# Padding two small resident tiles of an encoder trunk to multiples of 128 bytes

## The chip, the core and the metric

The kernel runs on one core of a Trainium2 chip. The metric is the device time of one execution in microseconds (us). Three runs of the kernel before took 3088.32, 3089.78 and 3091.51 us; their median, 3089.78, is its time. TensorE (PE in the profile) multiplies matrices, VectorE (DVE) and GpSimd (POOL) work element by element, ScalarE (ACT) applies functions and copies, SyncE (SP) issues most DMAs. On-chip tiles lie in SBUF, 128 partitions wide; results of TensorE land in PSUM.

## The reference, cut to what matters

Two layers over 256 tokens with 2048 features: a Conformer convolution module, then a bidirectional gated DeltaNet, each followed by a SwiGLU feed-forward of 5632 hidden units, with an RMSNorm ahead of each part and one at the end.

```python
def reference(x, ...):
    h = x
    for i in range(DEPTH):                      # 2
        hn = rmsnorm(h, mix_norm[i])
        if i == 0:
            mix = conformer_conv_module(hn, ...)   # pw1, GLU, 31-tap conv, LayerNorm, swish, pw2
        else:
            mix = gated_deltanet_bidir(hn, ...)    # one input product, scans both ways, out product
        h = h + mix
        h = h + swiglu_ffn(rmsnorm(h, ffn_norm[i]), w_gate_up[i], w_down[i])
    return rmsnorm(h, final_norm)

def swiglu_ffn(h, w_gate_up, w_down):
    gu = h @ w_gate_up
    gate, up = gu[..., :FFN_HIDDEN], gu[..., FFN_HIDDEN:]
    return (jax.nn.silu(gate) * up) @ w_down
```

Everything is float32.

## The kernel before, in words

**Products.** Features lie on partitions and tokens along the free axis, so an activation is a set of tiles of 128 features by 256 tokens. `products` (lines 163 to 196) computes blocks of 128 output features, over k-tiles of 128 input features. Weights come by DMA as `raw` tiles of eight k-tiles (line 149). For four k-tiles at a time ScalarE copies them into a `hi` tile of the type float32r (line 159), and VectorE writes the rest, `raw - hi`, into a `lo` tile (line 160). Activations are split in the same manner and lie as one tile `[hi | lo]` of 2 x 256 columns, 2048 bytes in a partition. For each k-tile TensorE then multiplies in one of two forms:

- *wide*: `lo` by the 256 columns of hi (line 184; line 187 in a block's first k-tile), `hi` by all 512 columns (line 185). Used by gate/up of both feed-forwards (activations `xs`, 88 blocks of 16 k-tiles in each layer), by down (`hs`, 16 blocks of 44), by pw2 (`y`, 16 blocks of 16) and by the DeltaNet's output product (`ys`, 16 blocks of 32).
- *narrow*: `hi` by hi, `hi` by lo, `lo` by hi, 256 columns each (lines 189, 190, 191). Used over `xs` by pw1 (32 blocks of 16) and the DeltaNet's input product (97 blocks of 16).

The weights are what TensorE holds; the activation tile is what streams through it, called the moving tile here.

**Order.** The tile framework's scheduler sets each engine's order and the waits. A wait orders a buffer's users: ScalarE, for one, writes a `hi` tile again once the last product that reads it is done. Four `hi` and four `lo` tiles go round, three `raw` tiles in the weights' pool and, during a feed-forward, three more in a pool of that phase, which every other chunk takes (lines 143 to 145).

**Where tiles lie.** Pools are laid out one behind the other in a partition, and tiles within a pool too, each rounded up to a multiple of 32 bytes. The first pool holds the constants (`cst_sb`, 1050 values, 4200 bytes, rounded to 4224) and the parameters of the features (`par_sb`, 499 values, 1996 bytes, rounded to 2016). 2016 is 32 more than a multiple of 64, so what follows begins at 32 modulo 64: the normed activations `xs`, the weights' pool (`raw`, `hi`, `lo`) and the first tiles of the small pool (`ss`, `rstd`, `warm`). `warm` (lines 244 to 247) is one value in a partition, 4 bytes rounded to 32: it brings what follows it back to 0 modulo 64. Its only use is to load a function's table on ScalarE early. Behind it lie `sq`, the residual stream `h` and the pools of each phase. Within the DeltaNet's pool a tile of 32 bytes, `rt`, makes most tiles behind it begin at 32 modulo 64.

Of the kernel before, what the change touches and what calls it, by code (L numbers as in the profile page):

```python
# [7 lines left out]
F32 = mybir.dt.float32  # L8
# [5 lines left out]
P = 128  # L14
# [9 lines left out]
CS = 4  # L24
NEG = -1.0e30
# PSUM banks
PSB = {"lin": 3, "sum": 1, "a": 1, "b": 2, "g": 1}
# [9 lines left out]
XB = 6  # L37
# taps of the depthwise convolution that GpSimd adds, by feature block
NPOOL = [15] * 12 + [14, 13, 6, 5]

# columns of the packed per-feature parameters
PAR = {}
# [9 lines left out]

# columns of the packed constants
CST = {}
# [12 lines left out]
def fv(ap, off, *dims):  # L67
    """A view of a tile by an offset and [stride, count] pairs over its free elements."""
    return bass.AP(ap.tensor, ap.offset + off, [list(ap.ap[0]), *[list(d) for d in dims]])


class Trunk:
    def __init__(self, ctx, tc, x, par, cst, pw1, pw2, win, wout, gu, dn, out):
        self.ctx, self.tc, self.nc = ctx, tc, tc.nc
        self.x, self.par_d, self.cst_d, self.out = x, par, cst, out
        self.pw1, self.pw2, self.win, self.wout, self.gu, self.dn = pw1, pw2, win, wout, gu, dn
        nc = self.nc
        pool = lambda name, **kw: ctx.enter_context(tc.tile_pool(name=name, bufs=1, **kw))
        self.cp = pool("const")
        self.xp = pool("acts")  # L80
        self.wp = pool("weights")
        self.sp = pool("small")
        self.ps = pool("psum", space=bass.MemoryType.PSUM)
        self.uid = 0
        self.pending = None
        self.ahead = self.more = None
        self.turn = False
        self.cst = self.cp.tile([P, NCST], F32, name="cst_sb")
        self.par = self.cp.tile([P, NRES], F32, name="par_sb")
        self.dram = pool("scratch", space=bass.MemoryType.DRAM)  # L90
        self.h_d = self.dram.tile([P, KD, S], F32, name="h_d")

    def new_h(self):
        """The residual stream on chip, in a pool of its own."""
        self.hs = ExitStack()
# [7 lines left out]
    def load_first(self, srcs):  # L103
        """The input and the first weights, in the order in which they are needed."""
        nc = self.nc
# [31 lines left out]

# [1 line left out]

    def raw_tile(self):  # L140
        """A chunk of weights; every other one from a phase that has room for more of them."""
        self.turn = not self.turn
# [3 lines left out]
    def raw_weights(self, src, k0, n):  # L146
        """n k-tiles of one column block."""
        raw = self.raw_tile()
        self.nc.sync.dma_start(raw[:, : n * P], src[:, k0 * P : (k0 + n) * P])
        return raw  # L150

    def halves(self, raw, i, n, pool=None):
        """k-tiles i to i + n as a high and a low part that float32r holds exactly."""
        nc = self.nc
# [8 lines left out]
    def products(self, srcs, kt, acts, wide=False, tags=("lin",), pool=None, order=None):  # L163
        """Blocks of 128 output features, k-tile by k-tile; acts: float32r tiles [P, hi | lo].

        order: of the k-tiles, within each CS of them."""
        nc = self.nc
# [37 lines left out]

# [1 line left out]

# [36 lines left out]
    def warm(self, func, after):  # L244
        """Loads a function's table on ScalarE, ahead of its use."""
        t = self.sp.tile([P, 1], F32, tag="warm", bufs=1, name=self.nm("warm"))
        self.nc.scalar.activation(t, after[:, :1], func)

# [9 lines left out]
    def norm_end(self):  # L258
        """The factor is traced behind the next product, whose result is the first to need it."""
        ss = [self.ss] if self.rest is None else [self.ss, self.rest]  # L260
        self.pending = lambda: self.rsqrt(self.token_sum(*ss), 1.0 / D, self.c("eps6"))

# [1 line left out]

    def conv_module(self, next_norm):
# [3 lines left out]
        with tc.tile_pool(name="conv", bufs=1, reuse_waits="tile") as cv:  # L269
# [27 lines left out]
            def add(key, t, n, last):  # L297
                """Sums over the channels, added up in PSUM."""
                if n == 0:
# [4 lines left out]
            def second(j):  # L304
                """The deviation from the first channels' mean, and its square's sum."""
                d = us[j]
# [64 lines left out]

            # mean = shift + dm: the first channels' deviations add up to nothing
            dm = new("dm", 1)
# [5 lines left out]
            lr = self.rsqrt(var, 1.0, self.c("eps5"), AF.Silu)  # L379
            # in the order in which VectorE and GpSimd get them done  # L380
            order = (0, 3, 1, 2, *range(4, KD))
# [21 lines left out]

# [1 line left out]

# [32 lines left out]

# [1 line left out]

    def deltanet(self, next_norm):
# [7 lines left out]
        G = NKH // 2  # L449
        # what the last heads leave early lies below what they need to the end  # L450
        with (tc.tile_pool(name="dn0", bufs=1, reuse_waits="tile") as d0,
# [23 lines left out]
        self.load_h(self.h_d)  # L475
        # the first lie within what dn0 leaves
        with (tc.tile_pool(name="out0", bufs=1, reuse_waits="tile") as o0,
# [15 lines left out]

    # tiles of the DeltaNet's pool: shape, number
    DN = {
# [33 lines left out]
    def dn_gates(self):  # L529
        """ln(beta) and the decays' sums within a block: as a token's scalars and along the tokens."""  # L530
        nc = self.nc
# [7 lines left out]
        V.tensor_scalar(m, y, 0.0, None, op0=ALU.max)  # L539
        # ln(1 + e) = 2 artanh(e / (2 + e))  # L540
        V.tensor_scalar(r, e, 2.0, None, op0=ALU.add)
# [41 lines left out]
    def short_conv(self, n):  # L583
        """Twice the SiLU of the five-tap convolution, of feature block n."""
        nc = self.nc
# [48 lines left out]
    def dn_front(self, g, qk):  # L634
        """Of four value heads, both ways: the masked, decayed products of keys with keys and with queries."""
        nc = self.nc
        xo, xd = self.d("xo"), self.d("xd")
        for h in range(2):
            q, k = qk[2 * h], qk[2 * h + 1]
            grams = []  # L640
            for x, tag in ((k, "kk"), (q, "kq")):
                ga = self.pst("g")
                # blocks of tokens ab, aa, bb, ba
                for i, (a, b) in enumerate(((0, 1), (0, 0), (1, 1), (1, 0))):
# [32 lines left out]
    def dn_lanes(self, xd):  # L677
        """Inverses of the 32 x 32 diagonal blocks of I + X, one block in a partition."""
        nc = self.nc
# [14 lines left out]
        at = lambda r, c: c * 32 + r  # L694
        # pairs of 1 x 1
        V.tensor_copy(fv(T, at(0, 1), (66, 16)), fv(L, at(0, 1), (66, 16)))
        # pairs of 2 x 2
        F = self.d("F")
# [8 lines left out]
        V.tensor_tensor(pj(T, 0, 3, (1, 2)), f(1, 0, (1, 2)), t0, op=ALU.add)  # L707
        # pairs of 4, 8 and 16
        for s in (4, 8, 16):
# [23 lines left out]
    def dn_inverse(self, g, xd, tt, tb):  # L733
        """The transposed inverses of the 128 x 128 triangular matrices from those of their diagonal blocks.

        One product serves both directions: what lies beside a diagonal block going forward and what lies
        beside it going backward are different blocks of one square. tt and tb hold the 32 x 32 inverses and
        their transposes; a matrix is counted by head and block of tokens (e), or by direction as well."""
        nc = self.nc
# [24 lines left out]

        # pairs of 32
        o = each(z32, lambda e: both(tt, e), 64)
# [7 lines left out]
        for d in range(2):  # L774
            V.transpose(fv(bl[rows(1 + d, 1)], 32 * d, (64, 8), (1, 32)), fv(o[rows(3 * d, 1)], 32 * d, (64, 8), (1, 32)))
        # pairs of 64
        o = each(z64, lambda e: bl[:, e * 64 : (e + 1) * 64], 64)
# [10 lines left out]
    def dn_heads(self, g, vs, xo, pb):  # L788
        """Four value heads: the solutions, and the normed outputs."""
        nc = self.nc  # L790
        blk = lambda t, m: t[:, m * P : (m + 1) * P]
        ot, os = [], self.d("os")
        for i in range(4):
            v = vs[i]
            # of pb: forward block a, forward block b, backward block a, backward block b
            inv = lambda m: blk(pb, 4 * i + m)
# [9 lines left out]

            # the first blocks (forward a, backward b), what they leave of the others, and those
            nc.scalar.copy(w1, two(w1, ((inv(0), blk(v, 0)), (inv(3), blk(v, 1)))))
# [3 lines left out]
            fa, ba, fb, bb = blk(w1, 0), blk(w2, 0), blk(w2, 1), blk(w1, 1)  # L812
            # ar: forward ab, aa, bb; backward aa, bb, ba
            o = self.pst("b")
# [94 lines left out]
def layout(i):  # L909
    """Arrays as the chip reads them: features on partitions, weights by blocks of 128 outputs."""  # L910
    import numpy as np
# [45 lines left out]
```

## Time and profile before

| What | Value |
|---|---|
| time, median of three runs | 3089.78 us |
| span of the profiled execution | 3092.0 us |
| TensorE busy | 2859.3 us, 92% of the span |
| VectorE busy | 2332.2 us, 75% |
| ScalarE busy | 1695.6 us, 55% |
| GpSimd busy | 1009.9 us, 33% |
| granted TensorE clock, mean over the span | 0.970 |
| bytes moved by DMA | 521.38 MB, mean 169 GB/s |

The profile was taken in an execution of its own, whose span from its first to its last instruction is 2.2 us longer than the median of the timed runs. A line such as "L185 PE MATMUL acc<-xs,hi 128*128 128x512 f32 x2816 | 982.0, 398 | 0.6 <-..." is a group: 2816 matmuls of line 185 that write `acc` and read `xs` and `hi`, 982.0 us busy in all, 398 ns the mean of one, then the engine's idle time just ahead of them and what ended it. Matmuls overlap each other, so their pitch (from one start to the next) is shorter than their duration; rates are read from starts.

### The profile page before, as it was taken

What the parts mean: (1) busy time and instruction counts of PE and PEld (TensorE: products, weight loads), DVE (VectorE), ACT (ScalarE), POOL (GpSimd) and SP (SyncE); (2) the same over time, 40 slices, a digit from 0 to 9 for tenths busy, and PEclk for the clock granted to TensorE, in tenths of its full rate; (3) what the DMA queues carried; (4) which work ended last, traced back from release to release, by engine and by line L of the source; (5) the groups of instructions that cost most, each with busy time, mean ns of one, the idle gap of its engine ahead of it and who ended that gap; (6) DMA issues with size and microseconds to landing.
All of it is one profiled execution on the core that took longest, in us unless ns stands there. A gap on an engine that the chain in (4) does not pass through costs nothing. (4 is left out here: it accounts for less than half of the span.)

```text
span 3092.0 us, 50294 instructions
## 1 busy us (share of the span) xinstructions
PE 2859.3 (92%) x18122; PEld 2566.7 (83%) x18122; DVE 2332.2 (75%) x3735; ACT 1695.6 (55%) x3449; POOL 1009.9 (33%) x1047
## 2 busy tenths in 40 slices
PE   7778799999999999878888889888999999999998
PEld 6777688888888889877888888888888888888887
DVE  8999876666666667899899997985766666666555
ACT  6665555555555445654665456554545555555443
POOL 6777420000000111566667766562110000000111
PEclk9999899999999999999999999999999999999999
DMA  4333266555556665543544445456666555556664
GB/s 164 121 112 103 89 202 189 188 185 188 186 186 193 197 200 166 181 150 115 164 155 149 137 144 166 129 158 200 192 189 209 185 187 188 185 187 184 192 190 141
DMA packets 163866, 521.38 MB, mean 169 GB/s; under 512 B 18240, under 2 KB 34944, under 8 KB 163616
## 3 DMA queue, kind: packets, MB, share of 16 engines
q1 hardware_dynamic: 162320, 516.86, 52.7%
q8 instruction: 142, 2.33, 0.3%
q10 hardware_dynamic: 1296, 1.30, 0.1%
q14 instruction: 108, 0.88, 0.1%
HBM read 497.02 MB, written 21.07 MB: 168 GB/s over the span
## 5 line engine op out<-in xcount | busy, mean ns | idle before, releaser
L160 DVE TENSOR_TENSOR lo<-raw,hi 128x512 fp32r<-128x512 f32 x1764 | 1384.7, 788 | 644.6 <-ACT hi L159 638.3
L159 ACT CAST hi<-raw 128x512 fp32r<-128x512 f32 x1764 | 1085.9, 619 | 935.4 <-PE acc L185 692.8
L185 PE MATMUL acc<-xs,hi 128*128 128x512 f32 x2816 | 982.0, 398 | 0.6 <-ACT hi L159 0.6
L184 PE MATMUL acc<-xs,lo 128*128 128x256 f32 x2640 | 742.3, 281 | 0.0
L191 PE MATMUL acc<-xs,lo 128*128 128x256 f32 x2064 | 620.1, 302 | 96.4 <-DVE lo L160 95.6
L189 PE MATMUL acc<-xs,hi 128*128 128x256 f32 x2064 | 606.1, 295 | 31.1 <-ACT hi L159 18.9
L185 PEld LDWEIGHTS acc<-xs,hi 128*128 128x128 f32 x2816 | 517.7, 188 | 116.4 <-ACT hi L159 0.9
L190 PE MATMUL acc<-xs,hi 128*128 128x256 f32 x2064 | 605.2, 294 | 0.8 <-DVE xs L220 0.7
L191 PEld LDWEIGHTS acc<-xs,lo 128*128 128x128 f32 x2064 | 410.9, 200 | 128.8 <-DVE lo L160 123.0
L184 PEld LDWEIGHTS acc<-xs,lo 128*128 128x128 f32 x2640 | 499.0, 189 | 6.8
L185 PE MATMUL acc<-hs,hi 128*128 128x512 f32 x1408 | 486.8, 391 | 0.0
L189 PEld LDWEIGHTS acc<-xs,hi 128*128 128x128 f32 x2064 | 413.8, 201 | 37.1 <-ACT hi L159 21.1
L190 PEld LDWEIGHTS acc<-xs,hi 128*128 128x128 f32 x2064 | 413.9, 201 | 6.1 <-issue 4.3
L184 PE MATMUL acc<-hs,lo 128*128 128x256 f32 x1376 | 388.0, 282 | 0.0
L421 POOL TENSOR_TENSOR tg<-tg,rstd 128x256 f32<-128x256 f32 x88 | 65.0, 738 | 920.9 <-ACT tg L420 920.9
L185 PEld LDWEIGHTS acc<-hs,hi 128*128 128x128 f32 x1408 | 262.2, 188 | 53.4
L184 PEld LDWEIGHTS acc<-hs,lo 128*128 128x128 f32 x1376 | 259.9, 189 | 1.6
L230 POOL TENSOR_TENSOR sq<-h 128x256 f32<-128x256 f32 x59 | 55.0, 931 | 562.7 <-DVE h L432 383.9
L344 POOL TENSOR_TENSOR a<-a,m 128x256 f32<-128x256 f32 x218 | 196.3, 908 | 56.1 <-ACT m L343 45.8
L594 DVE SCALAR_TENSOR_TENSOR u<-t,par_sb,u 128x254 f32<-128x254 f32 (+1 forms) x256 | 178.8, 704 | 3.4 <-ACT u L590 2.2
L185 PE MATMUL acc<-ys,hi 128*128 128x512 f32 x512 | 177.8, 396 | 1.1 <-DVE ys L204 1.1
L184 PE MATMUL acc<-ys,lo 128*128 128x256 f32 x496 | 137.9, 286 | 1.8 <-ACT ys L203 1.6
(226 smaller groups left out, 3503.9 us busy)
## 6 DMA issues: line engine op xcount, KB each, us to landing
raw<-in_gu SPq DMA_DIRECT2D x352, 512.0 KB, 4.6
raw<-in_win SPq DMA_DIRECT2D x194, 512.0 KB, 3.8
raw<-in_dn SPq DMA_DIRECT2D x160, 512.0 KB, 3.6
raw<-in_pw SPq DMA_DIRECT2D x94, 512.0 KB, 3.3
raw<-in_wout SPq DMA_DIRECT2D x64, 512.0 KB, 3.7
a_d<-am SPq DMA_DIRECT2D x32, 384.0 KB, 2.7
ar<-a_d SPq DMA_DIRECT2D x32, 384.0 KB, 4.8
raw<-in_dn SPq DMA_DIRECT2D x32, 256.0 KB, 4.3
```

What stands on the lines that cost most here:

```text
L159: nc.scalar.copy(hi, r)
L160: nc.vector.tensor_tensor(lo, r, hi.bitcast(F32), op=ALU.subtract)
L184: nc.tensor.matmul(acc[:, S:], lo, a[:, :S], start=False, stop=False)
L185: nc.tensor.matmul(acc, hi, a, start=first, stop=last)
L189: nc.tensor.matmul(acc[:, :S], hi, a[:, :S], start=first, stop=False)
L190: nc.tensor.matmul(acc[:, :S], hi, a[:, S:], start=False, stop=False)
L191: nc.tensor.matmul(acc[:, :S], lo, a[:, :S], start=False, stop=last)
L230: (nc.vector if last else nc.gpsimd).tensor_tensor(sq, h, h, op=ALU.mult)
L344: nc.gpsimd.tensor_tensor(acc, acc, m, op=ALU.add)
L421: nc.gpsimd.tensor_tensor(tg, tg, rstd, op=ALU.mult)
L594: nc.vector.scalar_tensor_tensor(u[:, lo:hi], t[:, lo + s : hi + s], w(i), u[:, lo:hi], op0=ALU.mult, op1=ALU.add)
```

## The change

The tile of the parameters is made 512 values wide (2048 bytes) and used through a view of its first 499; the tile of the warm-up is made 32 values wide (128 bytes), of which the first is written. The rest of the difference takes comments out.

```diff
@@ __init__
         self.cst = self.cp.tile([P, NCST], F32, name="cst_sb")
-        self.par = self.cp.tile([P, NRES], F32, name="par_sb")
+
+        self.par = self.cp.tile([P, -(-NRES // 32) * 32], F32, name="par_sb")[:, :NRES]
...
@@ warm
-        t = self.sp.tile([P, 1], F32, tag="warm", bufs=1, name=self.nm("warm"))
-        self.nc.scalar.activation(t, after[:, :1], func)
+        t = self.sp.tile([P, 32], F32, tag="warm", bufs=1, name=self.nm("warm"))
+        self.nc.scalar.activation(t[:, :1], after[:, :1], func)
```

In the built program every engine has the same instructions in the same order with the same waits and the same buffers; from line 89 on, line numbers are one higher. What differs is the addresses. Tiles ahead of `warm` move up by 32 bytes, tiles behind it by 128. The table of starts, in bytes modulo 128 within a partition:

| Tiles | Before | After |
|---|---|---|
| `xs` (moving in gate/up, pw1 and the DeltaNet's input product) | 96 | 0 |
| `raw`, `hi`, `lo` of the weights' pool | 96 | 0 |
| `ss`, `rstd` | 96 | 0 |
| `raw` of a feed-forward's own pool | 0 | 0 |
| `hs` (moving in down), `ys` (moving in the DeltaNet's output product) | 0 | 0 |
| `y` (moving in pw2) | 64 | 64 |
| `hi`, `lo` of pw2's first three blocks, from a pool of their own | 64 | 64 |
| `sq`, `h`, and `tu`, `hf` of the feed-forwards | 0 | 0 |
| the DeltaNet's tiles behind `rt` (a start modulo 64) | 32 | 32 |

## The prediction

> **What bounds the kernel now.** I read the page's header first, then the busy time of each engine by stage, with the stages cut where TensorE's source tiles change: pw1, pw2, gate/up of layer 0, down, DeltaNet, wout, gate/up of layer 1, down.
>
> ```profile
> span 3092.0 us, 50294 instructions
> core 0: us, PE busy (x) PEld busy (x) DVE busy (x) ACT busy (x) POOL busy (x), PEclk, DMA share, GB/s
> 0.00:347.60 347.60, 258.76 (x1698) 233.32 (x1698) 323.70 (x466) 212.99 (x453) 251.32 (x311) 0.93 0.35 116
> 347.60:440.00 92.40, 92.31 (x512) 80.44 (x513) 79.36 (x131) 52.51 (x98) 27.26 (x31) 0.97 0.51 166
> 440.00:938.60 498.60, 497.80 (x2819) 431.92 (x2818) 320.19 (x574) 281.09 (x530) 34.22 (x46) 1.00 0.59 189
> 938.60:1183.00 244.40, 244.40 (x1409) 216.26 (x1408) 151.87 (x225) 117.69 (x193) 28.81 (x31) 1.00 0.64 192
> 1183.00:2132.00 949.00, 829.34 (x6361) 787.45 (x6360) 857.40 (x1341) 529.61 (x1255) 573.06 (x507) 0.94 0.48 154
> 2132.00:2335.40 203.40, 193.65 (x1100) 168.56 (x1099) 130.17 (x209) 103.00 (x198) 32.20 (x42) 0.97 0.61 191
> 2335.40:2832.70 497.30, 497.30 (x2819) 431.92 (x2818) 319.89 (x574) 281.26 (x530) 34.20 (x46) 1.00 0.59 189
> 2832.70:3077.50 244.80, 244.80 (x1411) 216.52 (x1410) 140.19 (x207) 116.51 (x192) 24.39 (x29) 1.00 0.60 178
> ```
>
> Four stages, both gate/ups and both downs, keep TensorE busy without a gap at a granted clock of 1.00. In pw1 and the DeltaNet VectorE is the fullest engine (323.70 of 347.60 us, 857.40 of 949.00 us). The chain of waits confirms it for the second gate/up, where nothing but the products stands on it. Its two-instruction pieces mark the start of each block of 16 k-tiles, since only there do two products of line 185 follow each other:
>
> ```profile
> by line: PE acc L185 66.4%; PE acc L184 31.5%; PE acc L187 2.0%; PE tsum L241 0.1%
> ...
> 2347.05 0.46 PE acc L185 x2
> 2352.71 0.46 PE acc L185 x2
> ...
> 2431.76 0.46 PE acc L185 x2
> ```
>
> 2347.05 to 2431.76 is 15 blocks: 5.647 us for 16 k-tiles, 352.9 ns for each. Block starts of the other wide products, from the timeline of TensorE, the first and the last of 13 blocks of down (44 k-tiles each), of 12 of wout (32) and of 9 of pw2 (16):
>
> ```profile
> 968.95 0.39 PE L185 MATMUL acc<-hs,hi 128*128 128x512 f32 x1
> ...
> 1167.50 0.39 PE L185 MATMUL acc<-hs,hi 128*128 128x512 f32 x1
> ...
> 2190.69 0.39 PE L185 MATMUL acc<-ys,hi 128*128 128x512 f32 x1
> ...
> 2324.05 0.39 PE L185 MATMUL acc<-ys,hi 128*128 128x512 f32 x1
> ...
> 377.77 0.39 PE L185 MATMUL acc<-y,hi 128*128 128x512 f32 x1
> ...
> 428.52 0.40 PE L185 MATMUL acc<-y,hi 128*128 128x512 f32 x1
> ```
>
> Down takes 198.55 us / 13 = 15.273 us a block, 347.1 ns a k-tile; wout 133.36 / 12 = 11.113, 347.3 ns; pw2 50.75 / 9 = 5.639, 352.4 ns. The same pair of instructions (512 and 256 columns, the same hi and lo tiles as weights) thus runs at two rates. What differs is the moving tile. By the table of starts hs and ys stand at 0 modulo 128 bytes, xs at 96 (32 modulo 64), y at 64. The page's groups show it too, in the mean of the 512-column product:
>
> ```profile
> L185 PE MATMUL acc<-xs,hi 128*128 128x512 f32 x2816 | 982.0, 398 | 0.6 <-ACT hi L159 0.6
> L185 PE MATMUL acc<-hs,hi 128*128 128x512 f32 x1408 | 486.8, 391 | 0.0
> ```
>
> The excess is no fixed cost at a block's edge. Within a block, starts of line 184 over xs lie unevenly (0.36, 0.34, 0.36 us), over hs evenly (0.35, 0.34, 0.35):
>
> ```profile
> 700.05 0.28 PE L184 MATMUL acc<-xs,lo 128*128 128x256 f32 x1
> ...
> 700.41 0.28 PE L184 MATMUL acc<-xs,lo 128*128 128x256 f32 x1
> ...
> 700.75 0.28 PE L184 MATMUL acc<-xs,lo 128*128 128x256 f32 x1
> ...
> 701.11 0.28 PE L184 MATMUL acc<-xs,lo 128*128 128x256 f32 x1
> ...
> 1100.05 0.28 PE L184 MATMUL acc<-hs,lo 128*128 128x256 f32 x1
> ...
> 1100.40 0.28 PE L184 MATMUL acc<-hs,lo 128*128 128x256 f32 x1
> ...
> 1100.74 0.28 PE L184 MATMUL acc<-hs,lo 128*128 128x256 f32 x1
> ...
> 1101.09 0.28 PE L184 MATMUL acc<-hs,lo 128*128 128x256 f32 x1
> ```
>
> **The change part by part.** No instruction is added, removed or moved; the padding itself is never written. The warm-up on ScalarE writes one element per partition as before, and the parameters' DMA brings the same 499 values per partition. What changes is where tiles begin.
>
> *Wide products over xs (gate/up).* xs goes from 96 to 0 modulo 128, the start that hs and ys have. A fast block of 16 follows from the two fast lengths: 15.273 us for 44 k-tiles and 11.113 for 32 differ by 4.160 us for 12 k-tiles, 346.7 ns each, and leave 0.020 us for a block's edge. So 16 × 0.3467 + 0.020 = 5.567 us. Against 5.647 that is 0.080 us a block; the gate/ups have 2 × 88 = 176 blocks: **14.1 us**, all on the chain, since TensorE has no gap there. The alternative, stage by stage, is an upper end: (498.6 + 497.3) / 2816 against (244.4 + 244.8) / 1408 is 353.7 against 347.4 ns, times 2816: 17.5 us. It also counts the stages' starts, so I take the blocks. The lower end of this term is nothing.
>
> Who would be late next? Everything that feeds a faster gate/up already feeds down at that rate: one hi, one lo per four k-tiles, 64% DMA share there against 59%. In gate/up VectorE is busy 320.19 of 498.60 us. ScalarE waits for TensorE, not the reverse, and hardly for the DMA:
>
> ```profile
> ACT hi L159 <- PE acc L185: 191.8, 341, 1.0
> ACT hi L159 <- DMA raw<-in_gu: 3.0, 1, 3.0
> ```
>
> So the whole gain should arrive. If the cover failed, the 7 us of each stage would turn into a wait of TensorE on line 159 or 160, and the term would shrink to nothing.
>
> *Weights hi and lo* go from 96 to 0 modulo 128. hs and ys run at 347 ns with weights at 96, so the fast rate doesn't need the move; that both begin at 0 is a pair which no sustained stage shows (rival 3). I take nothing.
>
> *pw2 over y.* y keeps its 64 modulo 128; only its weights move. The 13 blocks after the first three run as above, so between 0 and 13 × (5.639 − 5.567) = 0.9 us. I take 0, as its row stands at 0 modulo 64 already and is slow.
>
> *Narrow products over xs (pw1, DeltaNet).* Their moving operand and weights move as in gate/up, but they show no excess:
>
> ```profile
> 100.08 0.28 PE L189 MATMUL acc<-xs,hi 128*128 128x256 f32 x1
> 100.20 0.28 PE L190 MATMUL acc<-xs,hi 128*128 128x256 f32 x1
> 100.32 0.28 PE L191 MATMUL acc<-xs,lo 128*128 128x256 f32 x1
> 100.44 0.28 PE L189 MATMUL acc<-xs,hi 128*128 128x256 f32 x1
> ```
>
> Three products take 0.36 us, 120 ns each. The fast wide pair is 346.7 ns for 768 columns and two weight loads; the triple has the same 768 columns and three loads, 13 ns more, as much as one more load may cost. I take 0. Bounds: 129 blocks lose or gain at most what a wide block does, 129 × 0.080 = 10.3 us, and mostly beside VectorE, which is the fullest engine in both stages.
>
> *VectorE, ScalarE and DMA.* In gate/up every other raw tile comes from the phase's own pool, at 0 modulo 128, the others at 96. Both kinds are in these rows (minimum, median, maximum in ns):
>
> ```profile
> L159 ACT CAST hi<-raw x341: 604/622/623, 451.8 to 928.9; 128x512 fp32r<-128x512 f32 x171
> L160 DVE TENSOR_TENSOR lo<-raw,hi x341: 681/692/833, 452.5 to 929.7; 128x512 fp32r<-128x512 f32 x171
> ```
>
> The minima lie 18 and 11 ns below the medians, so an alignment effect of either sign is at most that, 3% on an engine that waits in the stages that end on TensorE. In the DeltaNet its own tiles keep their 32 modulo 64. I take 0, ± 4 us for pw1 and the DeltaNet, where 129 blocks × 4 lo tiles × 11 ns make 5.7 us, most of which lies beside other work.
>
> Sum: 3092.0 − 14.1 = 3077.9 us for the profiled execution's span. It is 2.2 us above the median of the three runs, 3089.78; the same step from the median gives 3075.7.
>
> [...]
>
> **The rivals.**
>
> 1. *The rate goes with something else than the start.* The slow stages also have short blocks: 16 k-tiles over xs and y, against 44 and 32 over hs and ys. And y, at 0 modulo 64, is slow, which speaks against a plain rule of 64 bytes. Against it: the excess lies inside the block, not at its edge, and TensorE shows no idle time there. Price: 0, so 3089.8. [...]
>
> 2. *More than gate/up gains.* If the narrow products or pw2 carry a hidden excess, up to 10.3 + 0.9 us more: down to 3064.5. Against it: 120 ns for 256 columns is already what the fast pair's sum suggests.
>
> 3. *Slower: equal starts are the slow ones.* The slow xs and its weights both begin at 96; the fast hs and ys begin at 0 against weights at 96, a different residue. If the moving stream and the weight load disturb each other when they begin alike, gate/up stays slow (0 against 0), and down and wout turn slow: 1408 + 448 k-tiles by (352.9 − 347.1) = 11 us, so 3101. It decides at the first block of down, at 15.53 us instead of 15.27. Against it: y, at 64 against 96, begins differently and is slow all the same.
>
> 4. *The change doesn't do what it says.* True in part: the DeltaNet's tiles behind its 32-byte tile stay at 32 modulo 64, y at 64 modulo 128. It is in the terms above.
>
> **How the numbers follow.** Forecast (gate/up turns fast, the rest stays): 0.62. Rival 1, or a mix that ends within it: 0.18. Rival 2: 0.09. Rival 3: 0.11. A measurement of this kernel tells about 0.2%, 6.2 us, from no change, so faster is 0.62 + 0.09 = 0.71, same 0.18, slower 0.11. The range runs from rival 2's end, 3064, to rival 1's with the runs' spread, 3092, and leaves out rival 3.
>
> **What would show it.** Right: blocks of gate/up 5.567 us apart, the 512-column product over xs at a mean of 391 ns as over hs, each gate/up some 7 us shorter, down still 15.27 us a block, pw1 and DeltaNet within 4 us. Rival 1: blocks at 5.647. Rival 2: L189 to L191 under 120 ns apart or the DeltaNet shorter by more than 4 us. Rival 3: down at 15.5 us a block. The prediction is wrong if gate/up turns fast and TensorE then waits for line 159 or 160.

## The result, and the profile after

| | Median | Lowest to highest | Runs |
|---|---|---|---|
| before | 3093.14 us | 3088.32 to 3098.38 | 20 |
| after | 3099.98 us | 3097.24 to 3106.05 | 20 |

The ratio after to before is 1.0022, 95% interval 1.0016 to 1.0029: the change costs 6.8 us. Of 20 runs of before the median lies 3.4 us above that of the first three.

The header of the page and the busy times of each engine by stage, of the kernel after (us, then busy time and instructions of TensorE, its weight loads, VectorE, ScalarE, GpSimd, then granted clock, DMA share, GB/s); the stages are gate/up, down, DeltaNet, wout, gate/up, down:

```profile
span 3097.8 us, 50294 instructions
core 0: us, PE busy (x) PEld busy (x) DVE busy (x) ACT busy (x) POOL busy (x), PEclk, DMA share, GB/s
438.80:937.40 498.60, 497.65 (x2820) 431.89 (x2819) 320.06 (x574) 280.63 (x530) 34.01 (x46) 1.00 0.60 189
937.40:1184.40 247.00, 247.00 (x1409) 216.42 (x1408) 151.70 (x225) 117.67 (x193) 28.79 (x31) 1.00 0.64 190
1184.40:2131.40 947.00, 836.95 (x6361) 793.91 (x6360) 855.05 (x1341) 530.10 (x1254) 571.51 (x507) 0.94 0.48 154
2131.40:2338.30 206.90, 196.38 (x1099) 168.49 (x1098) 129.99 (x209) 103.00 (x198) 32.20 (x42) 0.98 0.59 188
2338.30:2835.50 497.20, 497.20 (x2819) 431.93 (x2818) 319.82 (x574) 280.81 (x530) 33.99 (x46) 1.00 0.59 189
2835.50:3083.10 247.60, 247.60 (x1411) 216.70 (x1409) 140.23 (x207) 116.52 (x192) 24.42 (x29) 1.00 0.59 175
```

Both gate/ups are as long as before (498.60 and 497.20 us, against 498.60 and 497.30). Both downs, full of TensorE at a clock of 1.00 before and after, are longer: 247.00 and 247.60 us against 244.40 and 244.80. The DeltaNet and wout together take 1153.9 us against 1152.4.

The chain of waits of the kernel after, in the second gate/up (line 186 was 185), gives the blocks over xs, the first and the last of 21:

```profile
2349.86 0.46 PE acc L186 x2
...
2468.44 0.46 PE acc L186 x2
```

118.58 / 21 = 5.647 us, the same as before to the last digit. TensorE's timeline of the kernel after (start, us, line, operation; a piece "x2" of the 512-column product holds the last product of one block and the first of the next, as in the chain) gives down's blocks, 13 apart, and those of the output product, 12 apart:

```profile
968.05 0.62 PE L186 MATMUL acc<-hs,hi 128*128 128x512 f32 x2
...
1168.77 0.62 PE L186 MATMUL acc<-hs,hi 128*128 128x512 f32 x2
...
2192.05 0.63 PE L186 MATMUL acc<-ys,hi 128*128 128x512 f32 x2
...
2326.80 0.63 PE L186 MATMUL acc<-ys,hi 128*128 128x512 f32 x2
```

Down takes 200.72 / 13 = 15.440 us a block, where it took 15.273; the output product 134.75 / 12 = 11.229, where it took 11.113. This accounts for the change: 32 blocks of down × 0.167 = 5.3 us, some 14 steady blocks of the output product × 0.116 = 1.6 us, pw2 −0.3 us (below), some 6.6 us in all against 6.8 us measured.

Within a block of down, the starts of the `lo` product of the kernel after now lie 0.36, 0.34, 0.36 us apart, the unevenness that xs showed before, where hs had 0.35, 0.34, 0.35:

```profile
1100.21 0.28 PE L185 MATMUL acc<-hs,lo 128*128 128x256 f32 x1
...
1100.57 0.28 PE L185 MATMUL acc<-hs,lo 128*128 128x256 f32 x1
...
1100.91 0.28 PE L185 MATMUL acc<-hs,lo 128*128 128x256 f32 x1
...
1101.27 0.28 PE L185 MATMUL acc<-hs,lo 128*128 128x256 f32 x1
```

The page's groups of the kernel after (busy us, mean ns of one, then idle time just before and what ended it) say the same less sharply, since a mean duration holds overlap (over xs the two products of a pair have means of 398 and 281 ns, 679 in all, and pairs start 352.9 ns apart). The product over hs goes from 391 to 393 ns, that over xs stays at 398, and the two operations that split the weights don't move (787 and 619 ns, against 788 and 619):

```profile
L161 DVE TENSOR_TENSOR lo<-raw,hi 128x512 fp32r<-128x512 f32 x1764 | 1383.5, 787 | 652.7 <-ACT hi L160 644.1
L160 ACT CAST hi<-raw 128x512 fp32r<-128x512 f32 x1764 | 1085.2, 619 | 940.6 <-PE acc L186 700.3
L186 PE MATMUL acc<-xs,hi 128*128 128x512 f32 x2816 | 981.7, 398 | 0.7 <-ACT hi L160 0.7
...
L186 PE MATMUL acc<-hs,hi 128*128 128x512 f32 x1408 | 492.1, 393 | 0.0
```

So gate/up did not turn fast, and down and the output product turned slow. That is what rival 3 said.

### The profile page after: what moved, and what is told of

Read it like the earlier page. It is cut to its first block, busy times and chain, and to the rows that moved or that the text cites. A ratio compares the mean times of both kernels' runs of the same rounds, so it can differ in the third digit from the quotient of the medians.

```text
span 3097.8 us, 50294 instructions
## 1 busy us (share of the span) xinstructions
PE 2872.5 (93%) x18122; PEld 2571.6 (83%) x18122; DVE 2330.5 (75%) x3735; ACT 1695.7 (55%) x3449; POOL 1008.8 (33%) x1047
```

## The experiments

Two theories were set against each other. *Own start*: a wide product's rate goes with where the moving tile itself begins. *Distance*: it goes with how far the moving tile begins from the weights' tiles `hi` and `lo`, modulo 128 bytes. By the table of starts the distance (moving tile minus weights) was 0 for xs, 32 for hs and ys and 96 for y; the change moves xs and the weights together, so it is now 0 for xs, 0 for hs and ys, and 64 for y. Each kernel is the kernel before with the edit shown. Block times are means over all steady blocks, told from TensorE's timeline as above; the ends of a long stretch are shown for some. Where a kernel has a single time, the text says "one run"; there the block times carry the argument, since single times of the kernel before lie as much as 10 us apart.

### One padding alone

*The parameters' tile alone*, by 32 bytes, as the change does. It moves xs and the weights, hs and y by the same amount: own starts change, distances don't.

```diff
-        self.par = self.cp.tile([P, NRES], F32, name="par_sb")
+        self.par = self.cp.tile([P, NRES + 8], F32, name="par_sb")[:, :NRES]
```

> Only the parameters' tile is padded: xs and the weights begin at 0 modulo 128, hs and ys at 32, y at 96. Theory D (distance): the rate of a wide product is set by how far the moving tile begins behind the weights, modulo 128 bytes; 32 is fast, 0 and 96 are slow. Distances here are those of before (xs 0, hs and ys 32, y 96), so gate/up stays at 5.647 us a block, down returns to 15.27 us a block, and the time is that of before within 0.1%. Rival W (the weights' own start): long products are fast with weights at 96 and slow with weights at 0, so down is at 15.44 us a block as in the change, and the time 0.2% above before.

*The warm-up's tile alone*, by 96 bytes. It lies behind xs and the weights and ahead of hs, ys and y: own starts of xs stay at 96, distances become 0, 0 and 64.

```diff
-        t = self.sp.tile([P, 1], F32, tag="warm", bufs=1, name=self.nm("warm"))
-        self.nc.scalar.activation(t, after[:, :1], func)
+        t = self.sp.tile([P, 32], F32, tag="warm", bufs=1, name=self.nm("warm"))
+        self.nc.scalar.activation(t[:, :1], after[:, :1], func)
```

> Only the warm-up's tile is padded: xs and the weights stay at 96 modulo 128, hs and ys move to 96, y to 32. Theory D: distances are those of the change (xs 0, hs and ys 0, y 64), so down is at 15.44 us a block, the output product at 11.24, gate/up at 5.647, and the time 0.2% above before, as the change. Rival W: the weights stay at 96, so down stays at 15.27 and the time within 0.1% of before.

Measured: the first 3094.13 us, ratio to before 0.9999 (0.9990 to 1.0008); the second 3099.66, ratio 1.0021 (1.0012 to 1.0030). Two blocks of down, 13 apart, in the timeline of the kernel with the parameters' padding alone:

```profile
968.18 0.63 PE L185 MATMUL acc<-hs,hi 128*128 128x512 f32 x2
...
1166.73 0.63 PE L185 MATMUL acc<-hs,hi 128*128 128x512 f32 x2
```

and in that with the warm-up's padding alone:

```profile
969.37 0.62 PE L185 MATMUL acc<-hs,hi 128*128 128x512 f32 x2
...
1170.09 0.62 PE L185 MATMUL acc<-hs,hi 128*128 128x512 f32 x2
```

198.55 / 13 = 15.273 us and 200.72 / 13 = 15.440. Two blocks of gate/up, 80 apart, with the parameters' padding alone:

```profile
463.30 0.62 PE L185 MATMUL acc<-xs,hi 128*128 128x512 f32 x2
...
915.04 0.62 PE L185 MATMUL acc<-xs,hi 128*128 128x512 f32 x2
```

The first kernel moves every own start and no distance, and moves no time; gate/up stays at 451.74 / 80 = 5.647 us with xs at 0 modulo 128, where the prediction wanted it fast. The second kernel makes the whole loss of the change. Own start falls; distance stands.

### The other distances

*xs 32 bytes further from the weights*: 96 bytes behind the last xs tile push the weights and all tiles behind them up, so xs stands at distance 32 while hs, ys and y keep theirs.

```diff
-            xs = self.xp.tile([P, 2 * S], F32R, tag=f"xs{k}", name=self.nm(f"xs{k}"))
+            xs = self.xp.tile([P, 2 * S + 24 * (k == KD - 1)], F32R, tag=f"xs{k}", name=self.nm(f"xs{k}"))[:, : 2 * S]
```

> No padding of the change; 96 bytes behind the last xs tile instead. xs stays at 96 modulo 128, the weights move to 64, hs and ys to 96, y to 32: distance 32 for xs, hs and ys, 96 for y. Theory D: gate/up turns fast, 5.567 us a block instead of 5.647, down stays at 15.27, so 176 blocks by 0.080 us = 14 us less, 0.45% below before. Rival W (weights at 64, no longer off a multiple of 64): gate/up stays at 5.647 and down goes to 15.44, 0.2% above before. Rival B (blocks of 16 k-tiles are slow for another reason): gate/up stays at 5.647, time as before.

Measured: 3078.96 us, ratio 0.9949 (0.9935 to 0.9963). Of this kernel, two blocks of gate/up, 80 apart, in TensorE's timeline:

```profile
464.17 0.63 PE L185 MATMUL acc<-xs,hi 128*128 128x512 f32 x2
...
909.50 0.63 PE L185 MATMUL acc<-xs,hi 128*128 128x512 f32 x2
```

and the window of gate/up, in the columns of the stages above:

```profile
440.20:932.00 491.80, 490.80 (x2820) 431.02 (x2818) 320.46 (x574) 281.49 (x530) 34.58 (x46) 1.00 0.60 191
```

The waits of the same window (us in total, times, longest):

```profile
ACT hi L159 <- PE acc L185: 181.3, 300, 3.1
...
PE acc L185 <- ACT hi L159: 0.8, 1, 0.8
```

445.33 / 80 = 5.567 us, the block that the prediction had worked out from down and the output product, and the stage is 6.8 us shorter. ScalarE still waits for TensorE, 181.3 us, and TensorE for ScalarE once, 0.8 us: the cover holds. So the gain that was forecast is there, but it comes from the distance.

The narrow products' mean pitch (starts up to 130 ns apart) is 118.1 ns here, against 119.5 before and after. They carry an excess as well (more below), but the stage of pw1 (342.5 against 342.4 us) doesn't gain from it, and the DeltaNet's is 3.9 us shorter (945.2 against 949.1), where the kernels before and after, equal in that pitch, lie 2.0 us apart (949.0 and 947.0).

*Distance 96 for xs, 64 for hs and ys, 0 for y*: 8 floats behind the last xs instead of 24, and a warm-up tile of 16 floats.

> 32 bytes behind the last xs tile and 32 more for the warm-up: xs at 96 modulo 128, weights at 0, hs and ys at 64, y at 0. Distances: xs 96, hs and ys 64, y 0, none of them 32. Theory D: nothing is fast. xs at distance 96 is near what y shows there before, 5.64 us a block; y at 0 near what xs shows, 5.65; hs at 64 has no row yet, 15.3 to 15.5 (y at 64 in the change: 351 ns a k-tile, so 15.45). Time 0.1 to 0.3% above before. Rival W: weights at 0, so down at 15.44, gate/up unchanged, 0.2% above before. The run adds two points to the table rather than telling the two apart.

*Distance 64 for xs, 96 for hs and ys, 32 for y* (one run): 16 floats behind the last xs, a warm-up tile of 24.

> 64 bytes behind the last xs tile and 64 more for the warm-up: distances xs 64, hs and ys 96, y 32. It fills the table crosswise. Theory D: xs at 64 as hs at 64 elsewhere, 351 ns a k-tile, 5.62 us a block; hs at 96 as y and xs at 96 elsewhere, 352.4 ns, 15.51 us a block; y at 32 fast, 5.567. Rival T (each tile set has a rate of its own, whatever the distance): xs 5.647, hs 15.27 to 15.44, y 5.64.

Measured: 3100.72 us (ratio 1.0021, 1.0012 to 1.0031) and 3095.98 (beside 3093.9 of before). In the second, two blocks of down, 13 apart:

```profile
951.75 0.63 PE L185 MATMUL acc<-hs,hi 128*128 128x512 f32 x2
...
1151.95 0.63 PE L185 MATMUL acc<-hs,hi 128*128 128x512 f32 x2
```

200.20 / 13 = 15.400 us, where 15.51 had been expected; gate/up came to 5.640 instead of 5.62. The block over y came to 5.567, as the distance theory said; rival T, a rate fixed by the tile set, had 5.64 there and falls. The theory's order of the slow distances was wrong: xs runs alike at 64 and 96, and hs is quicker at 96 than at 64. With the runs above, every uniform distance in steps of 32 has been seen (us a block, ns a k-tile):

| Distance | xs, 16 k-tiles | hs, 44 | ys, 32 | y, 16 |
|---|---|---|---|---|
| 0 | 5.647, 352.9 | 15.440, 350.9 | 11.23, 350.9 | 5.647, 352.9 |
| 32 | 5.567, 347.9 | 15.273, 347.1 | 11.113, 347.3 | 5.567, 347.9 |
| 64 | 5.640, 352.5 | 15.437, 350.8 | 11.224, 350.7 | 5.617, 351.0 |
| 96 | 5.640, 352.5 | 15.400, 350.0 | 11.200, 350.0 | 5.639, 352.4 |

Of these four only 32 is fast for the wide products, whichever tile moves. y, slow before (96) and after (64), is as fast at 32 as xs. At 64 the blocks over hs, ys and y take two times in turn (over hs 15.349 and 15.524 us), and the table holds the mean of the two.

The narrow products have another best distance. Early in the DeltaNet they run without a gap over xs in every kernel. The same stretch of the kernel before (xs at distance 0) and of this one (64), in the columns of the stages:

```profile
1191.50:1218.00 26.50, 26.50 (x224) 26.50 (x223) 24.18 (x50) 14.95 (x25) 0.00 (x0) 1.00 0.56 180
```

```profile
1191.50:1218.00 26.50, 26.50 (x236) 26.50 (x235) 24.72 (x51) 14.78 (x27) 0.00 (x0) 1.00 0.60 193
```

At the same clock of 1.00 TensorE gets through 236 products instead of 224. In such stretches their starts lie 120.0 ns apart at distance 0, 118.0 to 118.7 at 32, 118.3 at 96 and 113.3 at 64. Over both stages the mean pitch falls from 119.5 to 114.8 ns, and still the DeltaNet takes 946.3 us against 949.1, 2.8 us less, beside the 2.0 us between before and after at one pitch.

### Every wide product at distance 32

The edit behind xs, and 64 bytes ahead of the y tiles:

```diff
-            xs = self.xp.tile([P, 2 * S], F32R, tag=f"xs{k}", name=self.nm(f"xs{k}"))
+            xs = self.xp.tile([P, 2 * S + 24 * (k == KD - 1)], F32R, tag=f"xs{k}", name=self.nm(f"xs{k}"))[:, : 2 * S]
...
-            var = new("var", 1)
+            var = cv.tile([P, S + 16], F32, tag="var", name=self.nm("var"))[:, :S]
```

> The kernel with 96 bytes behind the last xs tile, and 64 bytes more ahead of the y tiles: distance 32 for all four moving tiles (xs, hs, ys, y). Theory D: gate/up 5.567 us a block, down 15.27, output product 11.11, and now pw2 too: 13 blocks by (5.639 - 5.567) = 0.9 us less than with xs alone, so about 3078 us, 0.5% below before. If y is slow because of something else than its distance, its blocks stay at 5.64 and the time at 3079.

Measured: 3077.67 us (3075.42 to 3078.91), ratio to before 0.9947 (0.9934 to 0.9961), faster than the kernel before and the kernel after. Blocks over y in its timeline, 6 apart:

```profile
376.50 0.63 PE L185 MATMUL acc<-y,hi 128*128 128x512 f32 x2
...
409.90 0.63 PE L185 MATMUL acc<-y,hi 128*128 128x512 f32 x2
```

33.40 / 6 = 5.567 us instead of 5.639. Over 11 to 13 blocks that is about 0.9 us; against the kernel with the xs edit alone it can't be told from the runs' spread.

### Is it TensorE alone?

The two reads might meet on TensorE, or the distance might change how ScalarE's, VectorE's or the DMAs' accesses meet TensorE's. In the next pair the gate/up blocks behind the first read the first block's `hi` and `lo` again, so that no weights are loaded or split there, once at distance 0 and once at 32 (one run each; lines are two higher).

```diff
+            raws = [] if self.reuse else self.ahead.pop(0) if self.ahead else [self.raw_weights(s, k0, n) for s in srcs]
...
+                ws = self.kept[k0 + i] if self.reuse else [self.halves(r, i, m, pool) for r in raws]
+                self.kept[k0 + i] = ws
...
+                self.reuse = j > 0
```

> Starts as before. From the second block on, both gate/ups use the hi and lo tiles of their first block again, so 87 of 88 blocks of each layer load and split no weights: in those stages ScalarE and VectorE no longer write or read hi, lo and raw, and almost no DMA runs. The output is not the reference's. Theory P (the partner of the moving stream is TensorE's own weight load): the rate over xs stays at 5.647 us a block, distance 0 as before. Rival Q (the partner is ScalarE, VectorE or the DMA at work on the weights' tiles): the excess goes, 5.567 us a block.

> As the run before it, with 96 bytes behind the last xs tile: distance 32. The output is not the reference's. Theory P: 5.567 us a block, 0.080 less than at distance 0 under otherwise equal conditions. Rival Q: the same time a block as at distance 0.

The same stretch of gate/up, in the columns of the stages: the kernel before,

```profile
470.00:900.00 430.00, 430.00 (x2439) 373.53 (x2438) 274.34 (x495) 241.60 (x458) 28.04 (x38) 1.00 0.59 187
```

the kernel that uses its weights again at distance 0,

```profile
470.00:900.00 430.00, 430.00 (x2439) 373.51 (x2438) 80.82 (x190) 59.94 (x153) 28.61 (x39) 1.00 0.00 1
```

and that at distance 32:

```profile
470.00:900.00 430.00, 430.00 (x2474) 378.05 (x2473) 82.28 (x194) 60.87 (x155) 28.90 (x39) 1.00 0.00 1
```

Two blocks of each, 80 apart, in TensorE's timeline, at distance 0

```profile
462.35 0.62 PE L187 MATMUL acc<-xs,hi 128*128 128x512 f32 x2
...
914.08 0.62 PE L187 MATMUL acc<-xs,hi 128*128 128x512 f32 x2
```

and at 32:

```profile
462.76 0.63 PE L187 MATMUL acc<-xs,hi 128*128 128x512 f32 x2
...
908.09 0.63 PE L187 MATMUL acc<-xs,hi 128*128 128x512 f32 x2
```

The DMAs are gone (share 0.00 instead of 0.59), VectorE's and ScalarE's work fell to 30% and a quarter, and the blocks are still 451.73 / 80 = 5.647 us and 445.33 / 80 = 5.567 us. In this stretch TensorE alone touches `hi` and `lo`, so the effect lies between its own two streams, the moving tile and the load of the weights.

### Which load, and how fine

*The distance to `hi` alone, in steps.* Each `hi` tile is made 32 bytes longer, so the four begin 32 bytes apart: over xs the distance to `hi` runs through 0, 96, 64, 32 from chunk to chunk, over hs through 32, 0, 96, 64; the distance to `lo` stays at 0 and 32 (one run).

```diff
-        hi, lo = ((pool or self.wp).tile([P, CS * P], F32R, tag=t, bufs=XB if pool else HI, name=self.nm(t))[:, : n * P]
+        hi, lo = ((pool or self.wp).tile([P, CS * P + (8 if t == "hi" and not pool else 0)], F32R, tag=t, bufs=XB if pool else HI, name=self.nm(t))[:, : n * P]
```

> Each of the four hi tiles is 32 bytes longer, so that the four begin 32 bytes apart modulo 128; raw and lo tiles keep their starts modulo 128, and so do all moving tiles. Distance to hi by chunk of four k-tiles: xs 0, 96, 64, 32; to lo 0 throughout. Theory D with hi as partner: the four chunks of a gate/up block differ, the one at 32 runs at 347 ns a k-tile, the others at 351 to 353; down's chunks run at 32, 0, 96, 64 in turn, so down slows from 15.27 to about 15.4 us a block. With lo as the partner (the load during the 512-column product): nothing changes, 5.647 and 15.27. With raw, or what ScalarE and VectorE do there, as partner: nothing changes either.

Measured: 3084.08 us; down 15.302 us a block, gate/up 5.60, from these two blocks, 80 apart:

```profile
456.29 0.63 PE L185 MATMUL acc<-xs,hi 128*128 128x512 f32 x2
...
904.29 0.62 PE L185 MATMUL acc<-xs,hi 128*128 128x512 f32 x2
```

If `hi` alone decided, down would be near 15.40, with three chunks of four slow; if `lo` alone did, nothing would move. Neither holds: down hardly changed, and gate/up gained more than half of what distance 32 gives. The start of `hi` matters, and not alone.

*The two loads apart*, over xs: `hi` at distance 32 and `lo` at 0, then `hi` at 0 and `lo` at 32, by a small tile between them (one run each; lines are three higher, and one small memset on GpSimd is added).

```diff
+        if not hasattr(self, "gap"):
+            self.gap = self.wp.tile([P, 8], F32, tag="gap", bufs=1, name="gap")
+            nc.gpsimd.memset(self.gap, 0.0)
```

with the 24 floats behind the last xs in the first kernel; in the second without them, and with 24 floats in the gap.

> 96 bytes behind the last xs tile and 32 between the hi and the lo tiles: over xs distance 32 to hi and 0 to lo; over hs 64 to hi and 32 to lo. If the load of hi (during the product with lo, 256 columns) sets the rate: gate/up 5.567, down 15.44 us a block. If the load of lo (during the product with hi, 512 columns) sets it: gate/up 5.647, down 15.27. If both count: gate/up between, about 5.60, and down too.

> 96 bytes between the hi and the lo tiles alone: over xs and over hs distance 0 to hi and 32 to lo. If hi sets the rate: gate/up 5.647 and down 15.44 us a block. If lo sets it: gate/up 5.567 and down 15.27. If both count: 5.60 and 15.35. The chunks of e7 that had this pair over hs (mixed with others in a block) ran at 346.5 ns a k-tile, which speaks for lo.

Measured: 3084.57 and 3088.79 us, beside 3090.92 of before. Blocks of gate/up, 80 apart, in the first and then in the second kernel:

```profile
461.16 0.63 PE L188 MATMUL acc<-xs,hi 128*128 128x512 f32 x2
...
910.22 0.63 PE L188 MATMUL acc<-xs,hi 128*128 128x512 f32 x2
```

```profile
463.54 0.63 PE L188 MATMUL acc<-xs,hi 128*128 128x512 f32 x2
...
912.87 0.63 PE L188 MATMUL acc<-xs,hi 128*128 128x512 f32 x2
```

449.06 / 80 = 5.613 us and 449.33 / 80 = 5.617: over xs each load alone gives 0.034 and 0.030 of the 0.080 us. Over hs it is otherwise: at the second kernel's pair, 0 for `hi` and 32 for `lo`, a block of down takes 15.254 us, a little less than at 32 for both (15.273), and in the first kernel (64 and 32) 15.350. Over y the first kernel has 0 for `hi` and 96 for `lo`, neither of them 32, and these two blocks, 8 apart, are 44.43 / 8 = 5.554 us, less than at any distance of the table:

```profile
387.50 0.63 PE L188 MATMUL acc<-y,hi 128*128 128x512 f32 x2
...
431.93 0.63 PE L188 MATMUL acc<-y,hi 128*128 128x512 f32 x2
```

So no price for each load by its own distance gives all of these; how the two loads' distances go together counts too.

*Steps of 16 bytes.* xs is used from an offset within a longer tile: in layer 0 at distance 16 in the first eight k-tiles and 48 in the others, in layer 1 at 80 and 112. Four taps of one feature block in pw1 move from TensorE to VectorE beside it (one run).

```diff
+            o = {("mixn", 0): (4, 4), ("ffnn", 0): (4, 12), ("mixn", KD): (12, 12), ("ffnn", KD): (20, 28)}[wname, wi][k // 8]
+            xs = self.xp.tile([P, 2 * S + 32], F32R, tag=f"xs{k}", name=self.nm(f"xs{k}"))[:, o : o + 2 * S]
```

> The xs tiles are 128 bytes longer and used from an offset within: in gate/up of layer 0 distance 16 for k-tiles 0 to 7 and 48 for 8 to 15; in layer 1 distance 80 and 112. Four taps of pw1's feature block 12 go from TensorE to VectorE to make room. If the distance counts in steps of 32 bytes, 16 runs like 0 (353 ns a k-tile), 48 like 32 (347), 80 like 64 (351), 112 like 96 (352.5). If it counts byte by byte, 16 and 48 lie between their neighbours, 349 to 350 ns. Down and wout unchanged, 15.27 and 11.11 us a block.

Measured: 3092.84 us, with pw1 some 5 us longer, which uses up most of what gate/up gains; blocks of 5.587 us in layer 0 and 5.613 in layer 1. By k-tile the means over 88 blocks are about 346.6 ns at 16, 350.5 at 48, 348.9 at 80 and 353.0 at 112. The distance counts finer than in steps of 32: 16 is not like 0, nor 48 like 32.

## Why the prediction was wrong

**The step that failed** is the one that begins "What differs is the moving tile", and "xs goes from 96 to 0 modulo 128, the start that hs and ys have" with it. Two things differed between the slow and the fast stages of before, the moving tile's own start and its distance from the weights, and the prediction took the first. The parameters' padding alone, which changes own starts and no distance, gave a ratio of 0.9999 and blocks of 5.647 us. The 14.1 us of gate/up were nothing, because xs and its weights moved together.

**"Weights hi and lo … I take nothing"** failed for the same reason. It rested on hs and ys being fast with weights at 96; what made them fast was the pair, 0 against 96, and the change took it away. This is the missing term: 7 us on down and the output product, made by the warm-up's padding alone (1.0021, against 1.0022 for both).

**Rival 3 was the mechanism**, at a chance of 0.11, with the place right (the first blocks of down) and the price too high: 11 us and 15.53 us a block, against 6.8 and 15.440. The size came from 5.8 ns a k-tile, the difference between xs and hs; hs itself loses 3.8 ns, (15.440 − 15.273) / 44. Moving xs and hs to the same distance leaves 1.7 to 2.5 ns between them at distances 0, 64 and 96, so one stage's price can't be carried to another.

**What was held against rival 3 was misread.** That y, at 64 against weights at 96, took 352.4 ns shows that equal starts are not the only costly case. It was used as if it showed that they cost nothing. Had the distances 0, 32 and 96 of xs, hs and y been written beside their rates, "only 32 is quick" would have been as good an account of the rows as own starts, and a better one for y.

**What held.** pw2 came to 5.617 us a block from 5.639, within the 0 to 0.9 us worked out. The narrow products stayed at 119.5 ns, since xs stayed at distance 0 from its weights; but that they "show no excess" was misread. At distance 64 three of them take 340 ns where they took 360, less than the fast wide pair's 346.7, so the 13 ns were not the price of a third load. It cost the forecast nothing. pw1 and the DeltaNet within 4 us. The splitting operations stayed within 1 ns on average, as expected within their bounds. "Who would be late next": nobody, as the kernel with xs at distance 32 shows, which got 14.5 us by its medians (3093.51 − 3078.96) where 14.1 had been worked out.

**The range** ended at rival 1 and left rival 3 out, so it missed by 8 us. Part of it is the base: over 20 runs before stands at 3093.14 us, not 3089.78, itself above the range.

**Open** is the rule behind the distance. The runs show which of the four distances is fast, that both loads count over xs, and that 16-byte steps matter; not why 16 and 32 are better than 0 for the wide products and 64 for the narrow ones, why at the mixed pair (0 and 32) hs is fast and xs is not, nor why y is fastest at 0 and 96.

## What to carry to other kernels

Where products stand on the path, look at where the moving tile begins relative to the weights' tile modulo 128 bytes, not at whether either is "aligned": padding to round starts brought the two into a slow relation here (a block of down went from 15.273 us to 15.440). Before a difference between two stages is put down to one property, list every property in which they differ, here both starts and their difference, and check that the row which contradicts a rival contradicts it and not merely a stronger form of it. A padding of 96 bytes at the right place was worth 14.5 us here. The good distance was not one number, 32 for the wide products (5.567 us a block over xs, 5.640 to 5.647 at the others) and 64 for the narrow ones (113.3 ns apart, 118.0 to 120.0 at the others); try a few such paddings between the two tiles and read the pitch of the products.

## What the hardware showed unexpectedly

Back-to-back pairs of products with 512 and 256 columns, with the same instructions, order and clock of 1.00, ran at 347 to 353 ns a pair by where their operands lie relative to each other: over xs 5.567 us for 16 pairs at a distance of 32 bytes, 5.647 at 0. With the DMAs gone (share 0.00 instead of 0.59) and most of VectorE's and ScalarE's work (the weights used again), the two numbers were the same, so these 0.080 us lie between the moving stream and the weight load of TensorE. Products of 256 columns in a row, each with its own weight load, started 120.0 ns apart at a distance of 0 and 113.3 at 64.

The two kernels that use their weights again differ by 0.080 us a block, 1.4%, with the distance of xs changed from 0 to 32 and its own start left at 96. Where the two reads meet, no run shows.
